# The second layer's tree of scores: 128x128 tiles against 32-column tiles on the four quarters of the array

## The chip, the cores and the metric

The kernel runs on one core of one Trainium2 chip. A core has four engines that compute: TensorE (PE in the profile; its loads of the stationary operand are shown as PEld), VectorE (DVE), ScalarE (ACT) and GpSimd (POOL); SP issues the DMAs. The metric is the device time of one execution in microseconds (us), the median of several runs; lower is better.

## What is computed

Four layers follow each other on 512 tokens of width 1024 (with 256 tokens of context in the first two): an attention and convolution layer, a gated linear recurrence in two directions, and two blocks of another model with their feed-forward layers. All is fp32. The change lies in the second layer, the recurrence, whose core in the reference is this, for one direction (the other runs on the flipped sequence, and both outputs are added):

```python
def hgrn2_scan(q, k, v, log_f, s0, with_outputs):
    """Chunkwise S_t = diag(f_t) S_{t-1} + k_t v_t^T, o_t = S_t^T q_t along axis 2."""
    ...
    b = jnp.cumsum(log_f, axis=3)
    ...
        def step(s, xs):
            q_n, k_n, v_n, b_n, qi_n, ks_n, d_n = xs
            o_inter = jnp.einsum('bhcd,bhde->bhce', qi_n, s)
            diff = b_n[:, :, :, None, :] - b_n[:, :, None, :, :]
            w = jnp.exp(jnp.where(tri, diff, -jnp.inf))
            scores = jnp.einsum('bhcd,bhsd,bhcsd->bhcs', q_n, k_n, w)
            o_n = o_inter + jnp.einsum('bhcs,bhse->bhce', scores, v_n)
            return d_n[..., None] * s + jnp.einsum('bhcd,bhce->bhde', ks_n, v_n), o_n
```

There are 8 heads with keys and values of 128. A score of query t and key s in the same block is a product over 128 channels, each weighted by the gates f between s and t.

## The kernel before

**The stage.** `layer1_mix` (line 851) does the layer head by head, with the channels of a head on the 128 partitions and the 512 tokens along the free dimension. `project(h)` (line 892) makes a head's queries `q`, gates `F`, keys `K` (both directions beside each other, `[128, 512, 2]`) and values `vT` from the layer's input: five projections of 24 matmuls with 512 moving columns, of which three also have 24 with 256 columns for the context. The operands of these are split in two parts (`wp_h`, `wp_l`, `a_h`, `a_l`), so that they run as fp32r; each weight block needs one copy on ScalarE (line 244) and one subtraction on VectorE (line 250), with four buffers each. `gate(h)` (line 919) is a sixth projection.

**The scan of a head.** `scan(h)` (line 929) has the 512 tokens in four blocks of 128. Inside a block the scores are found by a tree of seven levels (lines 973 to 999). At level l the tokens are taken in runs of m = 2^l; keys and queries of sibling runs meet, and `K` and `Q` have been multiplied by the gates up to the border between them. For each level

- ScalarE copies the keys that face each sibling to `km` (line 978),
- TensorE multiplies them with the queries (lines 979 to 982): four matmuls of 128x128, one for each block, fp32, into one bank of PSUM (`a`, four banks in turn),
- VectorE copies, out of the 128x128 scores of each block, those that belong to this level to `sc` by a mask (`copy_predicated` with `tree[:, l]`, line 983); the diagonal has been put there first (lines 956 to 961),
- VectorE multiplies `K` and `Q` with the gates for the next level, and pairs of gates with each other (lines 986 to 990).

So at each level the whole 128x128 square is computed, and the mask keeps a part of it. Behind the tree come the state of the blocks (`kTs`, `S`, lines 1001 to 1008: six updates of `S` on VectorE) and the output (line 1010 on): for each block a matmul with `sc` and one with the state `S` of each direction, into one bank; then its mean square (`m_sq` with `ones`), the norm, and the gate.

**What sets the order.** Each engine works through its own list in order. `scan(h)` and the projections of head h + 1 (and the gate of head h - 1) are generators that are advanced in turns (lines 1032 to 1042), so that the projections' matmuls stand between the steps of the tree; the tile framework then sets the final place of each instruction and the waits. Head 7 has three gates beside it instead of projections with context.

**Names in the rows.** `m_` is this stage's pool: `m_km`, `m_k`, `m_qp` (= `Q`), `m_f`, `m_sc`, `m_S`, `m_ks` (the sum of both directions' keys, for the diagonal), `m_kT`, `m_vn`. `a` and `mm` are banks of PSUM. An fp32 matmul stands in the trace as two records, and so does its weight load. L318 is the line of the helper `matmul`, L250 that of `tt`, L244 of `copy`, L266 of `stt`. Another place of the kernel already uses quarters of the array: the conditioning of the first layer (line 430), fp32 matmuls of 32 stationary and 256 moving columns with `tile_position=(0, 32 * k)`, four beside each other.

Of the kernel before, what the change touches and what calls it, by code (L numbers as in the profile page):

```python
# [18 lines left out]
L = 512  # L19
LC = 256  # L20
# [27 lines left out]
def _constants():  # L48

    c = {}  # L50
    p = np.arange(128)
    t = np.arange(L)
    d = p % 64
    j = d % 32
    freqs = (np.float32(10000.0) ** (-np.arange(16, dtype=np.float32) / np.float32(16))).astype(np.float32)
    pos = np.where((d // 32)[:, None] == 0, t[None] // 64, t[None] % 64).astype(np.float32)
    ang = (pos * freqs[j % 16][:, None]).astype(np.float32)
    c["cos1"] = np.cos(ang.astype(np.float64)).astype(np.float32)
    c["sin1"] = (np.sin(ang.astype(np.float64)) * np.where(j < 16, -1, 1)[:, None]).astype(np.float32)
    i = np.arange(128)  # L60
    neg = np.float32(-1e30)
    left = np.where(i[None] >= i[:, None], np.float32(0), neg)
    right = np.where(i[None] <= i[:, None], np.float32(0), neg)
    zero = np.zeros((128, 128), np.float32)
    c["mask1"] = np.concatenate([left, zero, right], 1)
    dist = 384 + i[:, None] - np.arange(512)[None]
    w = (dist >= 0) * ((dist <= 128) * 1.0 + (dist % 4 == 0) + (dist % 16 == 0))
    c["mask2"] = np.where(w > 0, 8.0 * np.log(np.maximum(w, 1.0)), neg)
    inv = (np.float32(500000.0) ** (-(np.arange(8, dtype=np.float32) * np.float32(2) / np.float32(16)))).astype(np.float32)
    c["rope2"] = np.stack([  # L70
        np.where(d < 16, inv[d % 8], 0), np.where(d < 8, -1.0, 1.0),
        np.where(p < 64, 1.0, -1.0), np.where(p < 64, -1.0, 1.0),
    ], 1)
    c["steps"] = np.broadcast_to(np.concatenate([np.arange(9), 8 * np.arange(64)]), (128, 73))
    c["sel"] = np.tile(np.eye(32, 2), (4, 1))
    dm = np.zeros((128, 16))
    dm[112 + np.arange(16), np.arange(16)] = 1
    c["dm"] = dm
    c = {k: np.ascontiguousarray(v.astype(np.float32)) for k, v in c.items()}
    lev = np.arange(7)[None, :, None]  # L80
    tree = ((i[:, None, None] >> lev) == ((i[None, None] >> lev) ^ 1)).astype(np.int32)
    c["tree"] = tree.reshape(128, -1)
    return c

# [104 lines left out]
class Prog:  # L189
# [628 lines left out]
    def layer1(self):  # L818
        nc, tc = self.nc, self.tc
        with ExitStack() as es:  # L820
            Y = Alloc(es, tc, "y1", {"y": (8, L)}, side="right")
            with ExitStack() as e1:
                K = Alloc(e1, tc, "k1", {n: (1, w) for n, w in (
                    ("tree", 896), ("zero", LC))})
                ys = self.layer1_mix(e1, K, self.xs1, Y)
            self.block2()
            N = Alloc(es, tc, "n1", {
                "cb": (1, L), "a1": (1, L), "a2": (1, L), "sq": (2, L), "m2": (1, 256), "r": (2, 256),
                "t": (1, 256), "gb": (2, 8)})
            ps = self.psum(mm=5, z=3)  # L830
            for k in range(KT):
                nc.sync.dma_start(out=self.x[k], in_=self.keep[k])
            xs2 = [self.split(self.a1, y, L) for y in ys]
            lng, lnb = self.vec("ln_g", 8, 16), self.vec("ln_b", 8, 16)
            pre, stats = self.prenorm(es, ps, "norm_mix_pre", 0)
            g = self.vec("norm_mix_pre", 0, 8)
            sc, bi = N("gb", 8), N("gb", 8)
            self.mul(sc, lng, g)
            self.mul(bi, lnb, g)

            def emit(k, s, x):
                pre(k, s, x, sc, bi)

            use, done = self.deepnorm(N, ps, self.x, self.mods[1], emit)
            self.out_products(ps, lambda m: self.I["wo_c"][m], xs2, PARTS[:2], use, done, spare=(Alloc(es, tc, "w5", {"h": (1, 1024), "l": (1, 1024)}), 1))
            for k in range(KT):
                self.ts(self.x[k], self.x[k], lng[:, k:k + 1], ALU.mult, lnb[:, k:k + 1], ALU.add, nc.gpsimd if k % 2 else None)
            stats()
        self.es1.close()

    def layer1_mix(self, es, K, xs, Y):
        nc, tc = self.nc, self.tc
        A = Alloc(es, tc, "m2", {
            "q": (2, L), "f": (2, 1024), "k": (2, 1024), "fc": (4, LC), "kc": (4, LC), "vT": (1, LT), "vn": (2, LT),
            "g": (3, L), "ks": (1, L), "sc": (2, L), "qp": (2, 1024), "km": (2, L), "e": (2, LC), "kT": (2, 384), "S": (4, 512), "gs": (2, L),
            "sq": (1, L), "r": (1, L), "t": (1, L),
        })
        ps = self.psum(mm=4, a=4)
        tree = self.load(K, "tree", self.I["tree"]).rearrange("p (l c) -> p l c", l=7)
        lb, oml = self.lower  # L860
        zero = K("zero")
        nc.gpsimd.memset(zero, 0.0)
# [66 lines left out]
        def scan(h):  # L929
# [23 lines left out]
                )  # L953
                self.mul(kd, kd, e)
            yield
            p = ps("a")
            for b in range(4):
                s = slice(b * 128, (b + 1) * 128)
                self.matmul(p[:, s], ks[:, s], q[:, s])
            sc = A("sc")  # L960
            self.mul(blk(sc), blk(p), self.idn.unsqueeze(1).to_broadcast([128, 4, 128]))
            S = [A("S", shape=[128, 4, 128]) for d in range(2)]
            orders, kTs = ((0, 1, 2, 3), (3, 2, 1, 0)), []

# [8 lines left out]
            for l in range(7):  # L973
                m = 1 << l
                nb = L // (2 * m)

                km = A("km")
                self.copy(km, mixed(K, m, 0))
                p = ps("a")
                for b in range(4):  # L980
                    s = slice(b * 128, (b + 1) * 128)
                    self.matmul(p[:, s], km[:, s], mixed(Q[:, s], m, 1))
                nc.vector.copy_predicated(
                    out=blk(sc), mask=tree[:, l].unsqueeze(1).to_broadcast([128, 4, 128]), data=blk(p)
                )
                T = F[:, :2 * nb].rearrange("p (b two) d -> p b two d", two=2)
                for x, j in ((K, 0), (Q, 1)):
                    x = mixed(x, m, j)
                    self.mul(x, x, across(F, nb, j).unsqueeze(3).to_broadcast([128, nb, 2, m]))
                self.mul(F[:, :nb], T[:, :, 0], T[:, :, 1])  # L990

                if l < 2:
                    kTs.append(turned([fc[l][1][:, i * 128:(i + 1) * 128] for i in range(2)]))
                elif l < 4:
                    p = ps("a")
                    for i in range(2):
                        self.matmul(p[:, :128], kTs[l - 2][:, i], vn[:, 4 + i], i == 0, i == 1)
                    self.copy(S[l - 2][:, orders[l - 2][0]], p[:, :128])
                yield
# [895 lines left out]
```

## Time and profile before

| | |
|---|---|
| median of 3 runs | 2109.29 us (2106.44 to 2116.51) |
| profiled execution, its own time | 2109.53 us |
| its span, first to last instruction | 2107.7 us |
| TensorE, VectorE, ScalarE, GpSimd busy | 97%, 63%, 44%, 18% of the span |
| instructions | 30001 |
| the tree's matmuls (`m_km`), records | 448 in eight heads, between 507 and 882 us |

The page gives the busy time of each engine; a busy matmul is one in flight, so matmuls that follow each other closely look like one busy stretch. The windows give the same for a stretch, with the granted clock of TensorE; the timeline gives instructions in order of time, with equal neighbours merged into one row, whose length runs from the first start to the last end; the view of a tile or a line gives the shortest, median and longest duration of its instructions. How close together instructions start is read from the starts of neighbouring rows.

### The profile page before, as it was taken

To read this page: it belongs to the slowest core of one execution; us is meant where nothing else is said; L and a number is where in the kernel's file an instruction comes from. 1 tells how busy PE (TensorE), PEld (TensorE's weight loads), DVE (VectorE), ACT (ScalarE), POOL (GpSimd) and SP (SyncE) were. 2 spreads that over 40 slices of the span, in tenths; PEclk is the share of its full clock that TensorE was granted. 3 is DMA by queue.
4 is the path that set the end of the run, shared out by engine and by line. 5 is a ranking of instruction groups with operands and counts; after the bars stand their busy time and mean duration, and the time that the engine had idled before them with its cause. 6 is when DMAs were issued, how large, how long until landed. Compare 5 with 4: busy or idle time off the path is not lost. (4 is left out here: it accounts for less than half of the span.)

```text
span 2107.7 us, 30001 instructions
## 1 busy us (share of the span) xinstructions
PE 2038.4 (97%) x11624; PEld 1736.8 (82%) x11624; DVE 1335.0 (63%) x2302; ACT 918.5 (44%) x1642; POOL 382.4 (18%) x383
## 2 busy tenths in 40 slices
PE   6999999999999999989999999999989999999997
PEld 4888888889888888878778888888887888888886
DVE  6775566786666666787765764544567786344455
ACT  2564334445444444446566554322346654322231
POOL 1111111344222222033111420100020131010011
PEclk9999999999999999999999999999999999999998
DMA  8344442322111111224332398532325322333231
GB/s 307 117 155 138 148 137 73 116 82 77 42 52 57 53 51 41 90 96 146 115 100 81 132 325 321 170 100 91 121 98 201 130 90 88 103 100 100 91 109 41
DMA packets 91662, 246.91 MB, mean 117 GB/s; under 512 B 20480, under 2 KB 29440, under 8 KB 91520
## 3 DMA queue, kind: packets, MB, share of 16 engines
q1 hardware_dynamic: 91520, 245.01, 34.9%
q8 instruction: 91, 1.49, 0.3%
q14 instruction: 51, 0.42, 0.1%
HBM read 209.84 MB, written 35.13 MB: 116 GB/s over the span
## 5 line engine op out<-in xcount | busy, mean ns | idle before, releaser
L244 ACT ACTIVATE wp_h<-wp_r 128x1024 fp32r<-128x1024 f32 (+2 forms) x243 | 250.9, 1037 | 409.9 <-PE mm L318 245.8
L250 DVE TENSOR_TENSOR wp_l<-wp_r,wp_h 128x1024 fp32r<-128x1024 f32 (+1 forms) x228 | 319.6, 1404 | 100.2 <-ACT wp_h L244 100.1
L318 PE MATMUL mm<-act_l,wp_h 128*128 128x512 f32 (+1 forms) x1008 | 380.0, 377 | 2.6 <-POOL act_l L250 2.6
L318 PE MATMUL mm<-act_h,wp_h 128*128 128x512 f32 (+1 forms) x1008 | 377.5, 375 | 2.5 <-ACT act_h L244 2.5
L318 PE MATMUL mm<-act_h,wp_l 128*128 128x512 f32 (+1 forms) x1008 | 377.8, 375 | 0.0
L318 PE MATMUL mm<-a_h,wp_h 128*128 128x512 f32 (+1 forms) x920 | 337.1, 368 | 5.2 <-ACT wp_h L244 3.2
L318 PE MATMUL mm<-a_h,wp_l 128*128 128x512 f32 (+1 forms) x920 | 330.5, 360 | 0.4 <-POOL wp_l L250 0.4
L318 PE MATMUL mm<-a_l,wp_h 128*128 128x512 f32 (+1 forms) x920 | 329.3, 358 | 0.7 <-DVE a_l L250 0.6
L318 PEld LDWEIGHTS mm<-act_l,wp_h 128*128 128x128 f32 x1008 | 193.4, 192 | 36.4 <-POOL act_l L250 3.3
L318 PEld LDWEIGHTS mm<-act_h,wp_h 128*128 128x128 f32 x1008 | 192.3, 191 | 35.3 <-ACT act_h L244 2.9
L318 PEld LDWEIGHTS mm<-act_h,wp_l 128*128 128x128 f32 x1008 | 193.2, 192 | 33.0 <-issue 1.0
L318 PEld LDWEIGHTS mm<-a_h,wp_h 128*128 128x128 f32 x920 | 174.4, 190 | 30.2 <-issue 3.6
L318 PEld LDWEIGHTS mm<-a_l,wp_h 128*128 128x128 f32 x920 | 174.5, 190 | 25.9 <-issue 2.3
L318 PEld LDWEIGHTS mm<-a_h,wp_l 128*128 128x128 f32 x920 | 174.3, 189 | 24.0 <-issue 0.7
L250 POOL TENSOR_TENSOR g_g<-g_g,g_u 128x512 f32<-128x512 f32 x44 | 61.3, 1395 | 551.7 <-DVE g_u L250 510.0
L318 PE MATMUL mm<-h_l,wp_h 128*128 128x512 f32 (+1 forms) x344 | 129.2, 376 | 0.6 <-DVE h_l L250 0.5
L318 PE MATMUL mm<-h_h,wp_h 128*128 128x512 f32 (+1 forms) x344 | 129.0, 375 | 0.5 <-ACT h_h L244 0.5
L318 PE MATMUL mm<-h_h,wp_l 128*128 128x512 f32 (+1 forms) x344 | 128.8, 374 | 0.0
L250 DVE TENSOR_TENSOR g_u<-mm,res_rr 128x512 f32<-128x512 f32 x44 | 30.3, 689 | 110.6 <-PE mm L318 110.6
L244 ACT ACTIVATE m_km<-m_k 128x512 f32<-128x512 f32 x56 | 37.6, 672 | 122.9 <-DVE m_k L250 101.4
L247 ACT ACT_TABLE_LOAD x60 | 77.0, 1283 | 1.8 <-PEq L1883 0.7
L318 PEld LDWEIGHTS mm<-h_l,wp_h 128*128 128x128 f32 x344 | 64.8, 188 | 13.5 <-DVE h_l L250 2.1
(498 smaller groups left out, 3898.1 us busy)
## 6 DMA issues: line engine op xcount, KB each, us to landing
wp_r<-w_gu SPq DMA_DIRECT2D x88, 512.0 KB, 3.5
wp_r<-w_c SPq DMA_DIRECT2D x40, 512.0 KB, 3.5
wp_r<-wada SPq DMA_DIRECT2D x32, 512.0 KB, 3.7
wp_r<-w_d SPq DMA_DIRECT2D x32, 512.0 KB, 3.5
wp_r<-w_ab SPq DMA_DIRECT2D x26, 512.0 KB, 4.7
od_d<-z_h SPq DMA_DIRECT2D x20, 512.0 KB, 3.8
od_d<-z_l SPq DMA_DIRECT2D x20, 512.0 KB, 4.5
wp_h<-od_d SPq DMA_DIRECT2D x20, 512.0 KB, 3.3
```

What stands on the lines that cost most here:

```text
L244: self.nc.scalar.activation(out=out, in_=in_, func=ACT.Copy, scale=scale)
L247: self.nc.scalar.activation(out=out, in_=in_, func=func, **kw)
L250: (eng or self.nc.vector).tensor_tensor(out=out, in0=a, in1=b, op=op)
L318: self.nc.tensor.matmul(out=out, lhsT=a, rhs=b, start=start, stop=stop)
```

## The change

The scores are computed in tiles of 32 keys by 32 queries. `scores` issues, for each block and each of the four runs of 32 keys in it, one matmul with these 32 keys as the stationary operand on quarter j of the array's columns, so that its result lands on partitions 32 j to 32 j + 31. For the diagonal and levels 0 to 4, sibling runs lie within the same 32 tokens; the queries are the same 32 tokens, and a block's scores of one level are 32 columns instead of 128. At level 5 the queries are the neighbouring 32, at level 6 the other 64.

The matmuls are issued in two groups a head: at level 2 those of the diagonal and of levels 0, 1 and 2 (64 matmuls into one bank), at level 6 those of levels 3, 4 and 5 (48 into one bank) and of level 6 (16 with 64 columns, into a second bank, `far`). Until then a level's keys and queries must be kept, since `K` and `Q` are changed in place: `km` has four buffers instead of two, and at levels 0, 1, 3, 4 and 5 the queries are copied by ScalarE too, to `qm` (three buffers). The diagonal and levels 0 to 4 are merged with masks of 32 columns in `sp`, `[128, 4 x 32]` (`own`: one product, five predicated copies of 128 columns). Ten copies then put `sp`, level 5 and `far` in their places in `sc` (`place`; four on VectorE, six on ScalarE). `sc` has one buffer instead of two, and the table of masks is 160 columns wide instead of 896.

```diff
--- before.py
+++ after.py
@@ -73,12 +73,13 @@
     ], 1)
     c["steps"] = np.broadcast_to(np.concatenate([np.arange(9), 8 * np.arange(64)]), (128, 73))
     c["sel"] = np.tile(np.eye(32, 2), (4, 1))
+    c["eye32"] = np.tile(np.eye(32), (4, 1))
     dm = np.zeros((128, 16))
     dm[112 + np.arange(16), np.arange(16)] = 1
     c["dm"] = dm
     c = {k: np.ascontiguousarray(v.astype(np.float32)) for k, v in c.items()}
-    lev = np.arange(7)[None, :, None]
-    tree = ((i[:, None, None] >> lev) == ((i[None, None] >> lev) ^ 1)).astype(np.int32)
+    lev, j = np.arange(5)[None, :, None], np.arange(32)
+    tree = ((i[:, None, None] % 32 >> lev) == ((j[None, None] >> lev) ^ 1)).astype(np.int32)
     c["tree"] = tree.reshape(128, -1)
     return c
 
@@ -821,7 +822,7 @@
             Y = Alloc(es, tc, "y1", {"y": (8, L)}, side="right")
             with ExitStack() as e1:
                 K = Alloc(e1, tc, "k1", {n: (1, w) for n, w in (
-                    ("tree", 896), ("zero", LC))})
+                    ("tree", 160), ("eye32", 32), ("zero", LC))})
                 ys = self.layer1_mix(e1, K, self.xs1, Y)
             self.block2()
             N = Alloc(es, tc, "n1", {
@@ -852,11 +853,12 @@
         nc, tc = self.nc, self.tc
         A = Alloc(es, tc, "m2", {
             "q": (2, L), "f": (2, 1024), "k": (2, 1024), "fc": (4, LC), "kc": (4, LC), "vT": (1, LT), "vn": (2, LT),
-            "g": (3, L), "ks": (1, L), "sc": (2, L), "qp": (2, 1024), "km": (2, L), "e": (2, LC), "kT": (2, 384), "S": (4, 512), "gs": (2, L),
+            "g": (3, L), "ks": (1, L), "sc": (1, L), "sp": (2, 128), "qp": (2, 1024), "km": (4, L), "qm": (3, L), "e": (2, LC), "kT": (2, 384), "S": (4, 512), "gs": (2, L),
             "sq": (1, L), "r": (1, L), "t": (1, L),
         })
         ps = self.psum(mm=4, a=4)
-        tree = self.load(K, "tree", self.I["tree"]).rearrange("p (l c) -> p l c", l=7)
+        tree = self.load(K, "tree", self.I["tree"]).rearrange("p (l c) -> p l c", l=5)
+        eye32 = self.load(K, "eye32", self.I["eye32"])
         lb, oml = self.lower
         zero = K("zero")
         nc.gpsimd.memset(zero, 0.0)
@@ -953,12 +955,39 @@
                 )
                 self.mul(kd, kd, e)
             yield
-            p = ps("a")
-            for b in range(4):
-                s = slice(b * 128, (b + 1) * 128)
-                self.matmul(p[:, s], ks[:, s], q[:, s])
-            sc = A("sc")
-            self.mul(blk(sc), blk(p), self.idn.unsqueeze(1).to_broadcast([128, 4, 128]))
+
+            def scores(p, keys, queries, n=32):
+                for b in range(4):
+                    for j in range(4):
+                        s = b * 128 + 32 * j
+                        nc.tensor.matmul(
+                            out=p[32 * j:32 * j + 32, b * n:(b + 1) * n], lhsT=keys[:, s:s + 32], rhs=queries(s, j),
+                            start=True, stop=True, tile_position=(0, 32 * j),
+                        )
+
+            w32 = [128, 4, 32]
+            sp, sc = A("sp"), A("sc")
+            todo = [(ks, lambda s, j: q[:, s:s + 32])]
+
+            def own(p, ls):
+
+                for i, l in enumerate(ls):
+                    src = blk(p[:, i * 128:(i + 1) * 128])
+                    if l < 0:
+                        self.mul(blk(sp), src, eye32.unsqueeze(1).to_broadcast(w32))
+                    else:
+                        nc.vector.copy_predicated(
+                            out=blk(sp), mask=tree[:, l].unsqueeze(1).to_broadcast(w32), data=src
+                        )
+
+            def place(src, r, c):
+
+                o, i = blk(sc)[r, :, c], blk(src)[r]
+                if r.start // 32 % 2:
+                    nc.vector.tensor_copy(out=o, in_=i)
+                else:
+                    self.copy(o, i)
+
             S = [A("S", shape=[128, 4, 128]) for d in range(2)]
             orders, kTs = ((0, 1, 2, 3), (3, 2, 1, 0)), []
 
@@ -976,13 +1005,33 @@
 
                 km = A("km")
                 self.copy(km, mixed(K, m, 0))
-                p = ps("a")
-                for b in range(4):
-                    s = slice(b * 128, (b + 1) * 128)
-                    self.matmul(p[:, s], km[:, s], mixed(Q[:, s], m, 1))
-                nc.vector.copy_predicated(
-                    out=blk(sc), mask=tree[:, l].unsqueeze(1).to_broadcast([128, 4, 128]), data=blk(p)
-                )
+                if l == 2:
+                    todo.append((km, lambda s, j, m=m: mixed(Q[:, s:s + 32], m, 1)))
+                elif l < 6:
+                    qm = A("qm")
+                    self.copy(qm, mixed(Q, m, 1))
+                    if l < 5:
+                        todo.append((km, lambda s, j, t=qm: t[:, s:s + 32]))
+                    else:
+                        todo.append((km, lambda s, j, t=qm: t[:, s + 32 - 64 * (j % 2):s + 64 - 64 * (j % 2)]))
+                if l in (2, 6):
+                    p = ps("a")
+                    for i, (k, f) in enumerate(todo):
+                        scores(p[:, i * 128:(i + 1) * 128], k, f)
+                    todo = []
+                if l == 2:
+                    own(p, (-1, 0, 1, 2))
+                elif l == 6:
+                    own(p, (3, 4))
+                    far = ps("a")[:, :256]
+                    half = lambda s, t: s // 128 * 128 + 64 - 64 * t
+                    scores(far, km, lambda s, j: Q[:, half(s, j // 2):half(s, j // 2) + 64, j // 2], 64)
+                    for j in range(4):
+                        r = slice(32 * j, 32 * j + 32)
+                        place(sp, r, r)
+                        place(p[:, 256:384], r, slice(32 * (j ^ 1), 32 * (j ^ 1) + 32))
+                    for t in range(2):
+                        place(far, slice(64 * t, 64 * t + 64), slice(64 - 64 * t, 128 - 64 * t))
                 T = F[:, :2 * nb].rearrange("p (b two) d -> p b two d", two=2)
                 for x, j in ((K, 0), (Q, 1)):
                     x = mixed(x, m, j)
```

On TensorE the tree stood as groups of four matmuls between projections. This is the start of a head in the middle of the stage (`m_ks` is the diagonal, `m_km` a level, `m_kT` the state of the context, `mm` the next head's projection):

```order
L318 MATMUL a<-m_qp,m_km 128x128 x4
L318 MATMUL mm<-a_h,wp_h 128x512
...
L318 MATMUL a<-m_q,m_ks 128x128 x4
...
L318 MATMUL a<-m_qp,m_km 128x128 x4
L969 MATMUL a<-idn,m_kc 128x128 x2
...
L318 MATMUL a<-m_qp,m_km 128x128 x4
L318 MATMUL a<-m_vn,m_kT 128x128 x2
```

Now the head has two groups, with nothing between their matmuls (`m_qm` are the copied queries):

```order
L963 MATMUL a<-m_q,m_ks 32x32 x16
L963 MATMUL a<-m_qm,m_km 32x32 x32
L963 MATMUL a<-m_qp,m_km 32x32 x16
L319 MATMUL a<-m_vn,m_kT 128x128 x2
L319 MATMUL mm<-a_h,wp_h 128x512
...
L963 MATMUL a<-m_qm,m_km 32x32 x48
L963 MATMUL a<-m_qp,m_km 32x64 x16
L319 MATMUL mm<-a_h,wp_h 128x512
```

Between the two groups stand the projections that stood between the groups of levels 2 and 6 before, 48 matmuls of 512 columns and 36 of 256.

On VectorE, the stretch between a head's last level and its state updates (`m_S`), before:

```order
L983 COPY_PREDICATED m_sc<-k_tree,a 128x512
L250 TENSOR_TENSOR m_qp<-m_qp,m_f 128x4x2x64
L250 TENSOR_TENSOR m_f<-m_f 128x8
L250 TENSOR_TENSOR m_qp<-m_f,m_q 128x1024
L250 TENSOR_TENSOR wp_l<-wp_r,wp_h 128x1024
L951 SCALAR_TENSOR_TENSOR m_e<-m_fc,k_zero 128x255
L250 TENSOR_TENSOR m_kc<-m_kc,m_e 128x256
L250 TENSOR_TENSOR m_k<-m_k,m_f 128x256x2
L266 SCALAR_TENSOR_TENSOR m_S<-m_S,m_f,a 128x128 x6
```

And now, from the same place on (`m_qp<-m_f,m_q` and what follows it belongs to the next head; 256x2 is its level 0, 128x2x2 its level 1):

```order
L979 COPY_PREDICATED m_sp<-k_tree,a 128x128 x2
L987 COPY m_sc<-m_sp 32x4x32 x2
...
L251 TENSOR_TENSOR m_qp<-m_f,m_q 128x1024
...
L251 TENSOR_TENSOR m_kc<-m_kc,m_e 128x256
L251 TENSOR_TENSOR m_k<-m_k,m_f 128x256x2
L251 TENSOR_TENSOR m_qp<-m_qp,m_f 128x256x2
L251 TENSOR_TENSOR m_f<-m_f 128x512
L251 TENSOR_TENSOR m_k<-m_k,m_f 128x128x2x2
L251 TENSOR_TENSOR m_qp<-m_qp,m_f 128x128x2x2
L267 SCALAR_TENSOR_TENSOR m_S<-m_S,m_f,a 128x128 x6
```

The products of the next head's levels 0 and 1 have moved ahead of the state updates; before, level 0's keys alone stood there, and the other three came behind them.

## Rows read from the trace of the kernel before

**Rows 1.** The page, busy time of the engines: us, share of the span, instructions.

```profile
PE 2038.4 (97%) x11624; PEld 1736.8 (82%) x11624; DVE 1335.0 (63%) x2302; ACT 918.5 (44%) x1642; POOL 382.4 (18%) x383
```

**Rows 2.** Windows: length, busy PE, PEld, DVE, ACT, POOL (count), clock, DMA.

```profile
605.23:656.95 51.72, 51.69 (x320) 45.46 (x319) 33.27 (x52) 21.22 (x36) 11.61 (x12) 1.00 0.17 51
...
sum 300.00, PE 299.77 PEld 263.18 DVE 192.60 ACT 125.28 POOL 67.42; mean PE 49.96 PEld 43.86 DVE 32.10 ACT 20.88 POOL 11.24
...
862.00:884.00 22.00, 21.70 (x118) 17.72 (x117) 21.56 (x36) 11.07 (x19) 2.59 (x2) 1.00 0.15 48
```

**Rows 3.** Timeline of TensorE around one level: start us, length us, instruction, count.

```profile
835.42 0.28 PE L318 MATMUL mm<-a_h,wp_l 128*128 128x256 f32 x1
835.54 1.07 PE L318 MATMUL a<-m_qp,m_km 128*128 128x128 f32 x8
836.36 0.48 PE L318 MATMUL mm<-a_h,wp_h 128*128 128x512 f32 x1
836.68 0.40 PE L318 MATMUL mm<-a_l,wp_h 128*128 128x512 f32 x1
836.91 0.40 PE L318 MATMUL mm<-a_h,wp_l 128*128 128x512 f32 x1
```

**Rows 4.** Timeline at the conditioning: first eight loads; first four matmuls; all sixteen.

```profile
85.58 0.16 PEld L430 LDWEIGHTS mc<-wp_r,sc 128*32 128x32 f32 x8
...
85.26 0.28 PE L318 MATMUL mc<-a_l,wp_h 128*128 128x256 f32 x1
85.38 0.28 PE L318 MATMUL mc<-a_h,wp_l 128*128 128x256 f32 x1
85.58 0.42 PE L430 MATMUL mc<-wp_r,sc 128*32 128x256 f32 x4
...
85.58 1.07 PE L430 MATMUL mc<-wp_r,sc 128*32 128x256 f32 x16
86.59 0.33 PE L656 MATMUL pt<-idn,m_P 128*128 128x128 f32 x1
```

**Rows 5.** Views of L430 and of two tiles: ns shortest/median/longest, first and last start.

```profile
L430 PEld LDWEIGHTS mc<-wp_r,sc x256: 106/109/110, 85.6 to 303.9; 128*32 128x32 f32 x128
L430 PE MATMUL mc<-wp_r,sc x256: 379/379/404, 85.6 to 304.2; 128*32 128x256 f32 x128
...
L318 PEld LDWEIGHTS a<-m_qp,m_km x448: 186/188/192, 507.4 to 881.8; 128*128 128x128 f32 x150
...
L318 PE MATMUL mc<-sel,adat_t x64: 165/251/272, 99.5 to 318.2; 128*128 128x2 f32 x64
```

**Rows 6.** One operation each: tile views (ns), then one head's groups (busy, mean ns).

```profile
L983 DVE COPY_PREDICATED m_sc<-k_tree,a x56: 725/748/768, 510.7 to 882.3; 128x512 f32<-128x512 int32 x56
L250 DVE TENSOR_TENSOR m_sc<-a,idn x8: 681/691/692, 509.5 to 862.1; 128x512 f32<-128x512 f32 x8
L244 ACT ACTIVATE m_km<-m_k x56: 654/670/702, 500.9 to 880.3; 128x512 f32<-128x512 f32 x56
L266 DVE SCALAR_TENSOR_TENSOR m_S<-m_S,m_f,a x48: 339/343/350, 543.3 to 887.7; 128x128 f32<-128x128 f32 x48
...
L244 ACT ACTIVATE m_S<-a 128x128 f32<-128x128 f32 x2 | 0.5, 264 | 0.0
L250 DVE TENSOR_TENSOR m_qp<-m_qp,m_f 128x512 f32<-128x512 f32 x7 | 4.7, 677 | 0.2 <-PE a L318 0.2
L250 DVE TENSOR_TENSOR m_f<-m_f 128x512 f32<-128x512 f32 x2 | 1.4, 682 | 0.0
```

**Rows 7.** Timeline around one head's state updates: VectorE, then TensorE at the output.

```profile
694.28 0.68 DVE L250 TENSOR_TENSOR m_k<-m_k,m_f 128x512 f32<-128x512 f32 x1
694.88 1.88 DVE L266 SCALAR_TENSOR_TENSOR m_S<-m_S,m_f,a 128x128 f32<-128x128 f32 x6
...
698.54 0.51 PE L318 MATMUL a<-m_qp,m_S 128*128 128x128 f32 x3
```

**Rows 8.** Timeline of TensorE at two matmuls of two columns.

```profile
99.49 0.28 PE L318 MATMUL mc<-sel,adat_t 128*128 128x2 f32 x2
```

## The prediction

> **What bounds the kernel now.** I read the page first: TensorE is busy for 97% of the span [rows 1]. Busy time of matmuls is modelled, so it proves little; the second view, the windows of the stage that the change touches (the scan of the second layer), says more. From 540 to 840 us TensorE is busy 299.77 of 300 us, and one head takes 51.72 us of which 51.69 are TensorE's, beside 33.27 of VectorE and 21.22 of ScalarE [rows 2]. The reader is to see that nothing but TensorE ends a step there: its order of work is fixed, it never waits, and the other engines wait for it. So in heads 0 to 6 a microsecond taken from TensorE is a microsecond of the span, until something else becomes late. Head 7 is different: it has no next head's projections beside it, and from 862 to 884 us VectorE is busy 21.56 of 22.00 us [rows 2]. There VectorE is the bound, or as good as that.
>
> **What a group of scores costs now.** An fp32 matmul is two pairs of weight load and matmul in the trace, so a level (four 128x128 matmuls) is eight pairs. The timeline shows one: it starts at 835.54, the projection's next matmul at 836.36, and the one behind that 0.32 later instead of the usual 0.23 to 0.24, since the first waits for the pipe [rows 3]. That is 0.82 + 0.085 = 0.905 us, or 0.113 a pair. A head has eight such groups (its own diagonal and seven levels): 7.24 us.
>
> **What a tiled group will cost.** The change makes of them 128 matmuls with 32 stationary columns, 256 pairs: 224 with 32 moving columns, 32 with 64. The trace has the same kind of matmul: the first layer's conditioning (L430) runs 32-column tiles on the four quarters with 256 moving columns. There four matmuls start within 0.02 us of each other, and sixteen are over in 1.07 us [rows 4]. One after another, at 0.113 for 128 columns, they would take 16 x 0.226 = 3.6 us. So the quarters do run side by side. From the last end (86.65) less a matmul's 0.379 and the 0.02 between the four [rows 4, 5], the last four start at 86.25; three steps from 85.58, with 0.024 more for the first (404 against 379), are 0.216 each, or 0.84 ns a column. For 32 columns that is 0.027 us, for 64 it is 0.054. Loads: 188 ns for 128 columns, 109 for 32 [rows 5], 0.82 ns a column, so 0.026 for 32, and the four first matmuls of L430 all take the same 0.40, so their four loads ran beside each other too. A pair of 128 columns costs 0.113 where its columns need 0.108; I add the same 0.006. A four then takes 0.033, and four starts 0.007 apart need 0.027, which fits in. I take 0.034, and 0.061 with 64 columns. Group one (the order shows 64 matmuls in a row) is 32 fours, 1.09 us; group two (48 and 16) is 24 x 0.034 + 8 x 0.061 = 1.31. Changing between whole array and quarters costs 0.08 going in (0.20 between starts at 85.38 where 0.12 is usual) and about 0.11 coming out (86.25 + 0.216 to 86.59) [rows 4]: 0.38 for two groups. Sum 2.78 us, against 7.24: TensorE is freed of **4.46 us a head**, 35.7 over eight. The low bound is 0.027 a four and 0.054, 2.32 in all, so 39.4 saved; the high bound is one tile after another (rival below). No row shows 128 pairs of this size in a row, only sixteen.
>
> **What comes on the other engines.** ScalarE gets five more copies of the queries a head at 0.670 and six placing copies, nearest to the 0.264 of a 128x128 copy out of PSUM [rows 6]: 3.35 + about 1.8 = 5.2 us, to 26.4 of some 47. VectorE loses seven predicated copies of 0.748 and a product of 0.691, 5.93 us, and gets six operations on 128 columns and four small copies at about 0.343 or less [rows 6]: 3.3, so 2.6 less, 30.7 of 47. Both stay hidden by the projections on the mean. Queued behind ScalarE's new copies are the splitting of weights and the sigmoids that empty the projections' banks; four buffers and four banks cover them. The table of masks that is loaded is smaller, once, before the stage: nothing. Packing six levels into one 128-column tile, and the wait of group two for keys and queries of levels 3 to 6, I cost at nothing: between the groups TensorE has 48 wide and 36 half projections, 48 x 0.235 + 36 x 0.118 = 15.5 us, against some 9 us of VectorE's chain (by the order eight products of 0.68 to 0.69, four smaller ones, three masked copies and one split of weights).
>
> **Where a wait comes.** The queries' product of a level had to wait until TensorE had read them. Now it waits for a copy on ScalarE, and the order shows what follows: VectorE does levels 0 and 1 of the next head before the six state updates, where only level 0's keys stood before. In the trace the keys' product is at 694.28, the updates run from 694.88 to 696.76, and the matmul that needs the last of them is the third of the output's, at about 698.77 (0.23 behind 698.54) [rows 7]: 2.0 us to spare. Put between are two query products of 0.677, one of gates at 0.682 and one of keys at 0.69 [rows 6, 7]: 2.73, with handing over 2.9. VectorE starts them when GpSimd's gates come, and these hang on a projection behind group two, as the output does, so the distance between them does not shrink. TensorE waits **0.9 us a head** at the output (bounds 0 and 2), in heads 0 to 5. Head 6 has less beside it; I take half a microsecond. In head 7, where VectorE is the bound, the gain is VectorE's 2.6 us, not TensorE's 4.46.
>
> **Sum.** 6 x (4.46 - 0.9) + 4.0 + 2.6 = 28.0 us. The profiled execution took 2109.53 (span 2107.7), 0.2 from the median 2109.29 of the three, so it may stand for them: 2109.5 - 28.0 = **2081.5 us**. Behind the stage the same work follows, shifted. The clock stays at its upper level of 2.4 GHz: the granted clock is 1.00 in these windows [rows 2], and the waits foreseen are under 1 us.
>
> **A rule that speaks against it.** Rows first: two matmuls of two columns on the whole array start 0.28 - 0.251 = about 0.028 apart [rows 5, 8], closer than their loads allow, but on the quarters starts are 0.007 apart [rows 4]. The Trainium skill, "TensorE: Matmul & The Clock Gate", section "Wait — 56ns, not 53.3ns?", says that starts never come closer than about 25 ns however few the columns. L430's starts disagree, and the measurement decides, for sixteen in a row. If the rule held in long rows of short matmuls, it would be the second rival.
>
> **Rivals.**
> *More waiting.* The quarters run side by side, but the copies cost more than averages show: ScalarE's queue is in order, and each new copy waits for VectorE. If TensorE loses 1.5 us more in each head, that is 12 us: 2093.5, and up to 2104. For it: VectorE's idle time before these steps was spent waiting for TensorE, so the slack is not known where TensorE is earlier. Against it: 15.5 us of projections between the groups.
> *A floor on each pair.* At 0.026 between any two starts, 256 pairs take 6.66 + 0.38 = 7.04 a head, 0.2 less than now: 2108, no change. Against it stand the four starts within 0.02.
> *One tile after another.* If four tiles with short columns don't overlap (a load and a drain for each, the queue feeding them one by one), 224 x 0.033 + 32 x 0.061 + 0.38 = 9.7 us a head, 2.5 more than now, 20 over eight: **2129, slower**. It decides from 0.0268 us a pair: (7.24 - 0.38) / 256. For it: L430's tiles stream eight times as long as these, so a feed of one pair each 0.03 us would be hidden there by the streams of 0.216. Against it: the first eight loads of L430 are over in 0.16 us, of which one takes 0.11 [rows 4, 5]: they were fed within 0.05, four of their matmuls too.
> That the groups are not built as described is out: the order has them in a row.
>
> **How the numbers follow.** Forecast (2069 to 2092) 0.60; more waiting (2092 to 2104) 0.15; below 2069 0.05; a floor 0.08; one after another 0.12. The range of 8 in 10 takes the first two and stops before the floor: 2069 to 2104. Half a per cent, 10.5 us, is about what a measurement of this kernel can tell from no change. Faster by more than that: 0.60 + 0.05 + 0.13 of the second case, 0.78. Within it: the rest of that case and the floor, 0.10. Slower: 0.12.
>
> **What would show it.** In the profile of the changed kernel a group of 128 pairs spans about 1.1 us from first start to the next kind of matmul, not 4; the head's period falls from 51.7 to about 48.2; TensorE shows a wait of about 0.9 us in front of the output's matmuls, ended by the state updates; in head 7 VectorE is still busy nearly throughout. A group of 3 to 4 us makes the sum wrong, and a wait of some microseconds ahead of group two would put ScalarE's copies in TensorE's place.

## The result and the profile after

| | kernel before | changed kernel |
|---|---|---|
| median, first comparison (4 runs each) | 2107.99 us | 2083.03 us (2080.92 to 2084.10) |
| median, second comparison (11 and 5 runs) | 2110.10 us | 2080.61 us |
| ratio of the two, first / second | | 0.9874 (0.9851 to 0.9897) / 0.9866 (0.9846 to 0.9887) |
| profiled execution, span | 2107.7 us | 2082.1 us |
| the stage, first to last head | 388.4 us | 360.4 us |

The change saves 25 to 29 us, 1.3%, and the forecast of 2081.5 us lies between the two medians. Single executions of one kernel differ by up to 16 us, so the stage alone tells more. I count it from the first transpose of a head's values to the mean square of the last head's output. The tile views of the changed kernel (ns shortest/median/longest, first and last start) give both ends; the last start is the second record of the last mean square, 0.45 behind the first:

```profile
L937 PE MATMUL a<-idn,m_vT x48: 270/272/328, 500.5 to 828.5; 128*128 128x128 f32 x48
L319 PE MATMUL a<-m_sq,ones x16: 592/601/697, 543.8 to 861.3; 128*128 128x512 f32 x16
```

From 500.48 to 860.88 this is 360.4 us. This length repeats within 0.15 us (below), so the change is worth **28.0 us in its stage**.

The page and the windows of one head in the middle and of head 7 from its first group on answer [rows 1] and [rows 2]:

```profile
PE 2008.2 (96%) x13160; PEld 1699.2 (82%) x13160; DVE 1307.2 (63%) x2318; ACT 955.9 (46%) x1730; POOL 386.9 (19%) x383
```

```profile
599.81:648.17 48.36, 48.10 (x511) 40.83 (x510) 29.97 (x54) 25.84 (x48) 11.70 (x12) 1.00 0.18 56
836.35:860.88 24.53, 23.01 (x365) 18.93 (x365) 19.81 (x42) 14.95 (x31) 2.97 (x2) 1.00 0.20 61
```

A head takes 48.36 us instead of 51.72. TensorE is still busy nearly throughout, VectorE has 3.3 us less and ScalarE 4.6 us more.

The timeline of TensorE in the same trace shows group one, group two (of the head before) and the output (start us, length us, instruction, count), as [rows 3] and [rows 7] did for a level and the output:

```profile
617.44 0.28 PE L319 MATMUL mm<-a_h,wp_l 128*128 128x256 f32 x1
617.65 1.03 PE L963 MATMUL a<-m_qm,m_km 128*32 128x32 f32 x96
618.52 0.68 PE L963 MATMUL a<-m_qp,m_km 128*32 128x64 f32 x32
619.13 0.50 PE L319 MATMUL mm<-a_h,wp_h 128*128 128x512 f32 x1
619.47 0.40 PE L319 MATMUL mm<-a_l,wp_h 128*128 128x512 f32 x1
...
647.85 0.40 PE L319 MATMUL mm<-a_h,wp_l 128*128 128x512 f32 x1
648.17 0.46 PE L963 MATMUL a<-m_q,m_ks 128*32 128x32 f32 x32
648.45 0.75 PE L963 MATMUL a<-m_qm,m_km 128*32 128x32 f32 x62
...
649.05 0.45 PE L963 MATMUL a<-m_qp,m_km 128*32 128x32 f32 x30
649.42 0.71 PE L319 MATMUL a<-m_vn,m_kT 128*128 128x128 f32 x4
...
682.54 1.03 PE L319 MATMUL a<-m_qp,m_S 128*128 128x128 f32 x4
683.41 0.38 PE L319 MATMUL a<-m_sc,m_vn 128*128 128x128 f32 x2
683.63 0.62 PE L319 MATMUL a<-m_qp,m_S 128*128 128x128 f32 x4
...
685.46 1.10 PE L937 MATMUL a<-idn,m_vT 128*128 128x128 f32 x6
```

Group one lasts from 648.17 to 649.42, 1.25 us, and group two from 617.65 to 619.13, 1.48. Within group one two starts take about 17 ns, so 8.5 ns a pair of load and matmul (8.9 from the first start to the last of all 128). At 682.54 four matmuls with the state last 1.03 us where the next four last 0.62: TensorE waits 0.4 us there, until VectorE's last state update is done. The transposes at 685.46 contain another wait of 0.3 (1.10 against 0.82 without it, shown below).

Adding up, for one head in the middle, the time from each TensorE start to the next by kind of matmul gives an account without remainder (us; the last three columns belong to experiments below):

| | before | changed | states first | group a level | same quarter |
|---|---|---|---|---|---|
| scores | 6.83 | 2.74 | 2.73 | 3.26 | 5.88 |
| projections | 37.78 | 37.78 | 37.78 | 38.76 | 37.76 |
| output, `m_S` | 1.85 | 2.26 | 1.85 | 1.85 | 2.25 |
| transposes, `m_vT` | 0.85 | 1.15 | 0.85 | 0.85 | 1.17 |
| `m_kT` with `m_vn` | 1.98 | 2.09 | 2.08 | 2.28 | 2.09 |
| the rest | 2.43 | 2.36 | 2.36 | 2.36 | 2.35 |
| head | 51.72 | 48.37 | 47.65 | 49.35 | 51.49 |

The projections' sum holds the late start behind eight groups before, and that around two groups now.

### The profile page after: what moved, and what is told of

Read it like the earlier page. It is cut to its first block, busy times and chain, and to the rows that moved or that the text cites. A ratio compares the mean times of both kernels' runs of the same rounds, so it can differ in the third digit from the quotient of the medians.

```text
span 2082.1 us, 33162 instructions
## 1 busy us (share of the span) xinstructions
PE 2008.2 (96%) x13160; PEld 1699.2 (82%) x13160; DVE 1307.2 (63%) x2318; ACT 955.9 (46%) x1730; POOL 386.9 (19%) x383
## 3 DMA queue, kind: packets, MB, share of 16 engines
q8 instruction: 103, 1.69, 0.3%
## 5 line engine op out<-in xcount | busy, mean ns | idle before, releaser
L251 DVE TENSOR_TENSOR wp_l<-wp_r,wp_h 128x1024 fp32r<-128x1024 f32 (+1 forms) x228 | 315.2, 1385 | 123.3 <-ACT wp_h L245 119.2
L251 DVE TENSOR_TENSOR g_u<-mm,res_rr 128x512 f32<-128x512 f32 x44 | 30.3, 689 | 110.5 <-PE mm L319 110.5
L319 PEld LDWEIGHTS mm<-h_h,wp_h 128*128 128x128 f32 x344 | 64.8, 188 | 14.6 <-ACT h_h L245 3.0
L251 POOL TENSOR_TENSOR act_l<-pn_h,act_h 128x256 fp32r<-128x256 f32 x64 | 57.5, 919 | 102.6 <-ACT act_h L245 102.2
```

Source lines behind the costliest of these rows:

```text
L251: (eng or self.nc.vector).tensor_tensor(out=out, in0=a, in1=b, op=op)
L319: self.nc.tensor.matmul(out=out, lhsT=a, rhs=b, start=start, stop=stop)
```

## Experiments

**What repeats.** The changed kernel once more, and the kernel before once more for a second trace (no edit):

> The changed kernel once more, beside the next three, so that they can be compared on one chip. Both theories: 2083 us within 2, and the same waits of TensorE in the second layer (0.31 us a head at the output).

> The kernel before once more, for a second trace. Theory that the second layer's stage repeats to 0.2 us while the rest of the kernel varies by some us between executions: from the first transpose of m_vT to the mean square of the last head 388.4 us again (360.4 in both traces of the changed kernel, so 28.0 saved there), and the first transpose not at 503.1 but somewhere from 499 to 503. Rival, that the stage itself varies: another length by 1 us or more.

Measured: the changed kernel took 2080.61 us again, with the wait at the output as in its first trace (`m_S` 2.24 to 2.26 us a head in the account). The stage took 388.4 us in the second trace of before and 360.3 in that of the changed kernel, the same to 0.1. The first transpose stood at 501.1 (before) and 503.1 (changed), the reverse of the first pair (503.1 and 500.5), and the part behind the last head varied by 4.9 us between the two traces of before. What the profiles differ by outside the stage is therefore not the change's.

**Neighbours on one quarter.** Only the order of a group's matmuls:

```diff
-                for b in range(4):
-                    for j in range(4):
+                for j in range(4):
+                    for b in range(4):
```

> The same tiled matmuls in another order: the four blocks of one quarter follow each other, then the next quarter, so that neighbours share a quarter. Theory that the gain comes from neighbours on different quarters running side by side: matmuls on one quarter take 0.033 us a pair one after another (0.06 with 64 columns), group one some 4 us instead of 1.25, group two some 5 instead of 1.49, 6 us a head more: 2125 to 2140 us, slower than before the change. Rival, that a short matmul takes about 10 ns wherever it goes, since that is how fast TensorE is fed: groups as now, 2083 us.

Measured: 2103.16 us, ratio 0.9968 (0.9950 to 0.9986); stage 381.1 us, 20.7 more than the changed kernel. Group one in the timeline:

```profile
656.05 0.80 PE L963 MATMUL a<-m_q,m_ks 128*32 128x32 f32 x29
...
658.00 0.78 PE L963 MATMUL a<-m_qp,m_km 128*32 128x32 f32 x29
658.72 0.71 PE L319 MATMUL a<-m_vn,m_kT 128*128 128x128 f32 x4
```

It lasts 2.67 us instead of 1.25, 20 ns a pair. Of eight starts in turn five are 26 to 32 ns apart and three 5 to 6. The rival is out: the same matmuls fed in the same number take twice as long, so the pace of 8.5 ns needs neighbours on different quarters. My number was too high: 6 us a head expected, 3.1 measured. Even so the order is faster than whole-array groups (scores 5.88 against 6.83 a head): of the 4.09 us a head that the scores lose by the change, 0.95 come without neighbours on different quarters.

**Twice as many, half as wide.** Every tiled matmul in two of half the columns:

```diff
-                for b in range(4):
+                for b, i in ((b, i) for b in range(4) for i in range(2)):
...
-                            out=p[32 * j:32 * j + 32, b * n:(b + 1) * n], lhsT=keys[:, s:s + 32], rhs=queries(s, j),
+                            out=p[32 * j:32 * j + 32, o:o + n // 2], lhsT=keys[:, s:s + 32], rhs=x[:, i * d:(i + 1) * d],
```

> Each tiled matmul is split in two of half the query columns (16, and 32 at level 6), so 512 pairs a head instead of 256, and as many columns in all. From the two kinds in the changed kernel's trace (39 ns for four pairs of 32 columns, 68 of 64) a four is 0.91 ns a column and 10 ns. Theory that columns set the pace: four pairs of 16 columns take 24.5 ns, 0.64 us a head more, 5 us in all, 2088 us, and group one takes about 1.6 us. Rival, that TensorE is fed a pair each 9.8 ns: group one takes 2.5 us, 2.3 us a head more, 2101 us.

Measured: 2152.94 us, ratio 1.0192 (1.0169 to 1.0214): neither; the stage takes 428.7 us, 68.3 more than in the changed kernel. The timeline of one group one, what TensorE waited for over the stage (us in total, times, longest), the instruction transfers from 676 to 681.2 us (count, MB, share), and a window behind a stop (length, busy PE, PEld, DVE, ACT, POOL, clock, DMA):

```profile
678.46 0.38 PE L965 MATMUL a<-m_qp,m_km 128*32 128x16 f32 x24
681.16 0.51 PE L965 MATMUL a<-m_qp,m_km 128*32 128x16 f32 x38 [2.32 <-issue]
681.60 0.71 PE L319 MATMUL a<-m_vn,m_kT 128*128 128x128 f32 x4
```

```profile
PE a L965 <- issue: 37.5, 16, 3.4
```

```profile
q8 instruction: 1, 0.02, 1.4%
```

```profile
759.00:762.00 3.00, 3.00 (x9) 2.32 (x8) 0.71 (x3) 0.28 (x2) 0.00 (x0) 0.51 0.03 5
```

Two things are to be seen. Up to the stop, pairs of 16 columns start 8.4 ns apart, as those of 32 do. So the moving columns don't set the pace of the changed kernel's groups of 32 columns; something that each pair costs alike does, at 8.4 ns a pair, and the fit of 0.91 ns a column was wrong below 64 columns. Whether that is the feeding of instructions or the load of 32 stationary columns, which every pair has too, no run here separates. And inside each of the 16 groups TensorE stops once, for 1.7 to 3.6 us from one start to the next, with no engine or data transfer as releaser ("issue"). Counted over all matmuls, the stops lie 382 to 384 pairs of load and matmul apart wherever they fall in a group (the last one 255), and some 160 to 253 short pairs had run before them. The trace's transfers of instructions tell more: in each of the 16 stops the transfer of exactly one block of 16 KB ends (in the one shown from 678.81 to 679.96), and TensorE goes on 1.2 to 1.6 us behind that end, whether the stop is short or long. Behind some of them the granted clock is at the lower level of 1.2 GHz (0.51 above, projections 0.43 us apart instead of 0.235), here after a group of short matmuls, a stop of 2.4 us and 1.1 us of matmuls.

**Halves in short groups.** The same halves, one group a level, so rows of at most 128 pairs:

> The split in halves of 16 columns again (512 pairs a head), but with one group a level, so that no row of tiled matmuls is longer than 128 pairs. Theory that the stops of 2 to 3 us in the split kernel come where TensorE runs through so many instructions in a row that the next ones have not been brought in: no such stop here, pairs 8.4 ns apart, 256 x 8.4 = 2.2 us a head more than the same groups with whole columns, at most 18 us: 2095 to 2108 us. Rival, that the stops come with the short columns or with the number of instructions in all: 14 stops or more as in the split kernel, 2140 us or more.

Measured: 2108.56 us, ratio 0.9992 (0.9979 to 1.0005), half a us above the theory's range; a head takes 51.09 us, 1.74 more than with whole columns in groups like these (the next run), where 2.2 were expected. What TensorE waited for from 500 to 900 us, all of it:

```profile
PE a L965 <- DVE m_qp L251: 1.4, 2, 1.1
PE a L319 <- ACT m_kT L245: 0.3, 1, 0.3
PE a L965 <- issue: 0.2, 1, 0.2
```

There is no stop of a microsecond without a releaser, although from 540 to 840 us 35 blocks of instructions come in (14 in the kernel before, 26 in the changed one, 33 in the split one with its longer heads). So neither short columns nor the number of instructions causes them, but a long row. The trace's own transfers fit that: a block is 16 KB (1.69 MB in 103 over the changed kernel), the split kernel runs 766 pairs in a head of some 57 us, in which 33 x 57 / 300 = 6.3 blocks come, 122 pairs each. Stops each 383 pairs are each third block (255 pairs are two). A row of 128 pairs uses up one block, and the next is there; in a row of 256 the next but one is not. The Trainium skill, "Runtime: NRT & Kernel Launch", section "Instruction fetch mechanics", says that each engine's instructions come in blocks of 16 KiB, 256 instructions, and that crossing into the next is mostly hidden. Block size and count agree with the trace; hidden it was in rows of up to 128 pairs, and not in the rows of 256 short ones. That TensorE waits for a block is read from the transfers in the 16 stops; why a block comes late in a long row is inferred from these counts, and rows of 256 pairs with 32 columns were not tried.

**One group a level.** No packing, no copies of the queries:

```diff
-                if l == 2:
+                if l < 5:
                     todo.append((km, lambda s, j, m=m: mixed(Q[:, s:s + 32], m, 1)))
...
-                if l in (2, 6):
+                if l < 6:
                     p = ps("a")
```

> One group of tiled matmuls at each level instead of two a head (the diagonal with level 0), so seven groups, and no copies of the queries. Theory that each change between whole array and quarters costs about 0.2 us (0.09 going in, 0.10 coming out, as in the trace of the changed kernel): five more groups are 1.0 us a head more, and the waits of 0.3 to 0.5 us a head that hang on ScalarE's copies go, so 0.5 to 1.0 a head, 2087 to 2091 us. Rival, that changing costs nothing worth naming and the five copies of the queries do: 2079 to 2083 us.

Measured: 2089.82 us, ratio 0.9897 (0.9877 to 0.9917); stage 368.0, 7.6 more. The account shows the price: scores and projections and `m_kT` take 1.69 us a head more for five groups more; the waits at the output and at the transposes (0.71) are gone; a wait of 0.16 for a copy of keys (`m_km`) is in it. Changing to the quarters and back costs (1.69 - 0.16) / 5 = **0.31 us**. The Trainium skill, "TensorEngine Tiling (Array Packing)", section "Key Properties", says that changing the tiling mode drains TensorE. The trace agrees in so far as starts are late on both sides of a group; that the array is empty by then it does not show.

**Copies twice.**

```diff
                     self.copy(qm, mixed(Q, m, 1))
+                    self.copy(qm, mixed(Q, m, 1))
```

> Each copy of the queries is made twice: ScalarE has 3.4 us a head more, about 29.8 of 48.4. Theory that the copies are hidden behind the projections in heads 0 to 6 and lie on the path only in head 7: 3 to 5 us more, 2085 to 2088 us. Rival, that each copy stands in a chain that TensorE waits for (level's copy, product, next level): 5 x 0.67 us in each head, 27 us more, 2110 us.

Measured: stage 360.3 us, nothing more, with ScalarE at 29.00 us a head instead of 25.84; 2084.45 us, ratio 0.9879 (0.9859 to 0.9898), which overlaps the changed kernel's. In heads 2 to 5 a head takes 48.38 us again, and no new wait stands ahead of a group: the copies as such are hidden there. The waits are not the same ones, though: the framework put the last state update one place later, so that the wait at the output is 0.73 us instead of 0.41 and the one at the transposes is gone. At the ends, too, the equal sum is made up of parts: head 6 takes 0.65 us more, head 1 0.26 more, and heads 0 and 7 take 0.65 and 0.40 less. The 3 to 5 us that I had expected in head 7 are not there.

**State updates first.** The edit sets VectorE's order alone; `last[0]` is the last state update of the head before:

```diff
-                    self.mul(x, x, across(F, nb, j).unsqueeze(3).to_broadcast([128, nb, 2, m]))
+                    with tc.issue_after(last[0]) if h and l < 2 and (l or j) else ExitStack():
+                        self.mul(x, x, across(F, nb, j).unsqueeze(3).to_broadcast([128, nb, 2, m]))
...
```

> VectorE's order alone: the six state updates stand ahead of the next head's products of levels 0 (queries) and 1 in all heads from the second on. Theory that the wait at the output is due to this order: the 0.31 us of TensorE there go in heads 1 to 6, 2081 to 2082 us, and the gap in front of the third m_qp,m_S matmul of a head falls from 0.42 to 0.11 us. Rival, that the state updates now wait for their products and VectorE loses that time ahead of the next group: a new wait in front of group one, 2083 to 2090 us.

> The order with the state updates first once more, on another chip perhaps. Theory that both waits (0.40 us at the output, 0.30 at the transposes of the values, a head) come from VectorE's order: the second layer from its first transpose to the last head's mean square is again 5 us shorter than in the changed kernel (355.3 against 360.4), and the time is 0.983 to 0.985 of the kernel before. Rival, that the first result was a good draw: within 2 us of the changed kernel, 0.986 to 0.988.

Measured: 2074.90 us, ratio 0.9840 (0.9820 to 0.9860), and 2078.49 us, 0.9847 (0.9821 to 0.9873); stage 355.4 and 355.2. One head's output and VectorE ahead of it in the second trace:

```profile
675.02 0.69 DVE L251 TENSOR_TENSOR m_k<-m_k,m_f 128x512 f32<-128x512 f32 x1
675.74 1.89 DVE L1058 SCALAR_TENSOR_TENSOR m_S<-m_S,m_f,a 128x128 f32<-128x128 f32 x6
677.54 0.69 DVE L251 TENSOR_TENSOR m_qp<-m_qp,m_f 128x512 f32<-128x512 f32 x1
...
679.64 0.62 PE L319 MATMUL a<-m_qp,m_S 128*128 128x128 f32 x4
...
682.15 0.82 PE L937 MATMUL a<-idn,m_vT 128*128 128x128 f32 x6
```

Both waits are gone (0.62 for 1.03, 0.82 for 1.10), the head takes 47.65 us, and TensorE has no wait over 0.15 us between 540 and 840 us. The size was more than twice what I had expected (0.71 us a head against 0.31), because the wait at the transposes hung on the same order. ScalarE's rows show it, two of the changed kernel and then two of this one:

```profile
684.19 0.66 ACT L245 ACTIVATE m_km<-m_k 128x512 f32<-128x512 f32 x1 [2.23 <-DVE m_k L251]
685.70 0.36 ACT L245 ACTIVATE m_vT<-mm 128x256 f32<-128x256 f32 x1
...
681.31 0.38 ACT L245 ACTIVATE m_vT<-mm 128x256 f32<-128x256 f32 x1
681.65 0.68 ACT L245 ACTIVATE m_km<-m_k 128x512 f32<-128x512 f32 x1
```

In the changed kernel ScalarE copies the second part of the values (685.70) behind the keys of the next head's level 3 (684.19), and these wait for VectorE, whose product for them stands behind the state updates. With the updates first the copy of the values (681.31) stands ahead of these keys (681.65): the order on ScalarE has moved with that on VectorE, and the run shows the effect of both together. In all the stage is 5.1 us shorter, in both traces alike. The intervals of the whole times overlap a little with the changed kernel's, but both medians are lower (2074.90 and 2078.49 against 2083.03 and 2080.61): of the kernel before, the changed one and this, this is the fastest.

**Placing copies later.** On top of the last one, the ten placing copies behind the transposed keys:

> As the run with the state updates first, and the copies that place the scores stand behind the transposed keys (m_kT) in ScalarE's order. Theory that in heads 0, 6 and 7 TensorE waits for m_kT because these copies are ahead of it: the waits of 0.66 us in head 0 and of 0.50 in head 7 get shorter, the second layer takes 354 us instead of 355.3, the whole 2073 to 2075. Rival, that the placing copies are then late for the output's matmuls with m_sc: waits there of 0.3 us a head or more, 358 us and 2077 or more.

Measured: 2079.58 us, ratio 0.9853 (0.9830 to 0.9876), stage 355.5. The wait of 0.50 us in head 7 is gone, that of 0.66 in head 0 is not, and the stage is no shorter: neither theory. What ends the last head then was not followed further.

**The first group alone.** The diagonal and levels 0 to 2 tiled, levels 3 to 6 whole with masks:

> Only the diagonal and levels 0 to 2 are tiled, in one group; levels 3 to 6 are whole 128x128 matmuls with masks as before the change. Theory that the parts add up: four levels at 0.905 us against one group of 1.25 and 0.2 for changing, 2.17 us a head, about 17 us less than before, and a part of the wait at the output stays: 2090 to 2095 us. Rival, that most of the gain (or of the waits) hangs on group two: under 10 us less than before, 2098 us or more.

Measured: 2102.55 us, ratio 0.9951 (0.9935 to 0.9968); stage 376.9, 11.5 less than before: by the stage between the two, by the time on the rival's side. A head takes 50.15 us: scores and projections 2.18 less than before, as the theory had it, but waits at the output (0.28 of 0.41) and at the transposes (0.30) are there without group two. So they belong to group one, whose copies and products stand ahead of the state updates.

## Why the prediction was right

**The quarters run side by side: right, the size at 32 columns by luck.** 0.034 us for four pairs was taken from the conditioning's columns; 8.5 ns a pair is what the groups run at. The reason was wrong: the split kernel shows 8.4 ns at half the columns, so up to 32 columns it is a limit of each pair, whatever its columns, which at 32 happens to be as large as the forecast. With 64 columns a pair took about 15 ns, as forecast. The Trainium skill, "TensorE: Matmul & The Clock Gate", section "Wait — 56ns, not 53.3ns?", has starts no closer than some 25 ns. Over 128 pairs on four quarters the trace shows 8.5, and even on one quarter 20 on average, so the measurement decides against that rival. The rival of one tile after another falls too: the groups cost 2.7 us a head, and even with neighbours on one quarter 5.9, not 9.7. One reading was a little off, and nothing in the sum hangs on it: the two matmuls of two columns [rows 8] start 0.026 us apart, not 0.028.

**Changing to quarters and back: too cheap.** I had 0.38 us a head; 0.31 a group is 0.62. This is the term that was mis-sized, by 0.24 of the 0.40 us that are missing a head (the other 0.16 was not traced to a term): TensorE was freed of 51.72 - 48.37 + 0.71 = 4.06 us a head, not 4.46. What I had left out is that the matmul behind the group starts late as well (0.335 instead of 0.235 us after group two), beside the 0.13 to 0.15 behind the last short one.

**The wait: right place and cause, size over twice too large.** 0.9 us at the output was forecast. It was 0.41 there, and 0.30 at the transposes of the values, which the prediction had not seen: 0.71 in all, near the forecast only because of a wait that was not forecast. VectorE in the changed kernel:

```profile
677.94 0.69 DVE L251 TENSOR_TENSOR m_k<-m_k,m_f 128x512 f32<-128x512 f32 x1
...
681.39 1.64 DVE L267 SCALAR_TENSOR_TENSOR m_S<-m_S,m_f,a 128x128 f32<-128x128 f32 x6
```

Two products of queries, one of gates and one of keys stand where the prediction put them, ahead of the state updates (from the keys' product at 677.94 to the first update at 681.39 there are 3.45 us, where [rows 7] had 0.6): 2.85 us more, 2.9 forecast. Two other things made the wait smaller. The distance from the keys' product to the output's third matmul, which was not to shrink, grew by 0.34 us (4.84 without the wait, 4.50 before), and the six updates took 1.64 us instead of 1.88. The run with the updates first shows that both waits come from the order of VectorE, the one at the transposes by way of ScalarE.

**Heads 6 and 7: wrong, in opposite directions.** By the mean squares of successive outputs, heads 0 to 5 gained 19.3 us (forecast 21.4), head 6 2.8 (4.0) and head 7 5.9 (2.6). Head 7 gained more than VectorE's 2.6 because VectorE now does its products of levels 0 and 1 within head 6: from the mean square of head 6 to that of head 7 it had 30.3 us of work before and has 23.9 now. With the updates first these products still lie within head 6, and head 7 takes the same (31.7 us). So VectorE was not the bound there any longer, and it was not busy nearly throughout (19.81 of 24.53 us from the first group on), which the prediction had given as a sign. Head 6 has a wait of 1.0 us for `m_kT`, which is gone with the updates first. The sum came to the forecast 28.0 by luck: heads 0 to 6 gave 3.3 us less than forecast, head 7 3.3 more.

**The other engines: right.** VectorE 29.97 us a head (30.7 forecast), ScalarE 25.84 (26.4). That the copies are hidden in the middle heads is shown by doubling them. The clock stayed at its upper level.

**"More waiting", the rival with 0.15**, did not come: no wait over 0.15 us stands ahead of a group in the middle heads, with the copies made twice either.

## What to carry to other kernels

Small matmuls on different column quarters are worth it even at 32 columns, if neighbours in the order go to different quarters: 8.5 ns a pair here against 20 on one quarter and 107 for a whole-array pair of 128 columns. Pack them, since each change costs 0.3 us, but keep a row near 128 pairs: rows of 256 pairs of 16 columns stopped for 1.7 to 3.6 us. And when a wait is moved from an engine's data to a copy, read in the new order what the freed instructions have overtaken; here putting six state updates back in front was worth another 5 us of stage.

## What the hardware showed that was not expected

- In rows of 256 short pairs TensorE stopped once each, after some 160 to 253 of them, for 1.7 to 3.6 us without a releaser in the profile, each 383 pairs or third block of instructions (37.5 us in 16 stops); rows of up to 128 pairs had no such stop. In each stop the transfer of one block of instructions ended 1.2 to 1.6 us before TensorE went on. After some stops the granted clock was 0.51.
- Pairs of 16 and of 32 columns on alternating quarters start equally far apart, 8.4 to 8.5 ns.
- On one quarter, pairs of 32 columns start 20 ns apart on average, in steps of 26 to 32 and 5 to 6 ns.
- The stage repeats within 0.15 us between executions (the order with the updates first on two chips), while the rest of this kernel varies by some microseconds.
